# Low halves of split weights on VectorE, gates and residual queued behind the normalised operand, key transposes ahead of the compressed keys

## The chip, the cores and the metric

The kernel runs on one core of a Trainium2 chip. The metric is the device time of one execution in microseconds (us), here the median of three.

## The reference, cut to what matters

Two models in a row act on 256 tokens of width 1024. The first has two layers of feed-forward, mixer (three kinds of attention heads side by side) and feed-forward; the second has one layer of a mixer of state-space and short-convolution branches ("part 2" here), and a mixture of 16 experts.

```python
for l in range(2):
    x = x + 0.5 * swiglu(rmsnorm(x, ffn1_norm[l]), ffn1_wg[l], ffn1_wu[l], ffn1_wd[l])
    h = rmsnorm(x, mix_norm[l]) @ w_in[l]
    ...
    x = x + concat(mla(h_a), nsa(h_b), diff(h_c)) @ w_out[l]
    x = x + 0.5 * swiglu(rmsnorm(x, ffn2_norm[l]), ffn2_wg[l], ffn2_wu[l], ffn2_wd[l])
x = rmsnorm(x, final_norm)
...
proj = rmsnorm(concat(meta, x), norm_mix) @ w_in_2      # z, xBC, dt, b, c, h
h = h + concat(ssd(z, xBC, dt), short_conv(b, c, h)) @ w_out_2
h = h + hier_moe(rmsnorm(h, norm_ffn), ...)
return rmsnorm(h, norm_final)[:, 16:]
```

Here `swiglu` is silu(x wg) times (x wu), times wd.

## The kernel before, in words

**Split weights.** The results are wanted at float32 accuracy. A weight unit of up to 1 MB is fetched by SyncE into a tile `st` (`load`, four buffers) and split in two halves of up to 128 x 1024 elements (`split`, L154 to L170). For each, ScalarE writes a high half `wh` (L167), and then VectorE or GpSimd writes the low half `wl` = `st` - `wh` (L168); six buffers each. TensorE multiplies with both (`mm`, `mm2`, `mm3`; all their matmuls carry line L99). The two letters of the argument `lo` say which engine makes the low halves: "v" VectorE, "p" GpSimd. The table `LOW` and some literals in the calls set it.

**Operands.** An activation operand is made the same way: a high part on ScalarE, a low part on VectorE (`operand`, L268 and L269). Squares for the norm are summed up along the way (`squares`: L281 on ScalarE, L286 and L288 on VectorE); `sum_squares` puts their sums over the partitions into `pss` by TensorE, and `inv_rms` and `rsqrt` (L299, L124 to L131) make `rr` of it in a chain of twelve short VectorE instructions.

**The mixer of the first model.** It begins with the operand of the feed-forward's output, the matmuls of w_in's nine units (`w_in_groups`), and the norms of the latent (`ckvn`, L634, then its transposes `ckvt`). `nsa_prepare` makes compressed keys and values (`kcmp`, `vcmp`, from `h1`, L780) and the transposed queries and keys (`qtb`, `ktb`, copied to `ks` and `kw`). The heads follow, and then w_out: four units in two halves each, a psum bank each, and two additions to `xT` (L957). Psum banks go by tag: here S has 3, T 2, O 1 and W 2.

**Part 2.** A string `PART2` sets the order in which the pieces are written: "z10" multiplies two of four units of z, "u" makes the norms and the operand `u` (`u_operand`: L1106 scales, ScalarE makes the high part, L1108 the low part), "z2" and "z3" the other two units, "d" the decays, "b0" to "b3" and "x0" to "x3" the units whose products go through a short convolution (`conv`: ScalarE L1195, three times L1197 on VectorE, tanh on ScalarE, L1200), "r" rewrites the residual (`residual_norm`, L1112). The gates of z (`z_gates`) are read out of psum by ScalarE, put through tanh (L1095), and finished on VectorE (L1096). The chain of the decays ends with L1169, for which the matmul `acp` waits. Later `y_norm` (L1366, L1371) and w_out_2's units w0 to w7 follow, with the first experts' weights prefetched between.

**What sets the order.** The programs of the engines are written piece by piece, and a scheduler of the tile framework orders each engine's instructions by its own estimate of when they can run. Between the engines only data and buffers make waits. `behind` (L138) tells the scheduler to issue what is inside after a given instruction.

Of the kernel before, what the change touches and what calls it, by code (L numbers as in the profile page):

```python
# [10 lines left out]
F32 = mybir.dt.float32  # L11
# [7 lines left out]
T = 256  # L19
NM = 16  # L20
# [14 lines left out]
         "h0 s1 s1 g0 s1 s2 s2 n0 c1 h1 s2 s3 g1 n1 s3 c2 h2 g2 s3 "  # L35
         "| c3 h3 p5 g3 n2 y a w6 t0 t1 p7 t2 w0 n3 t3 % w1 p4 w5 w2 w4 p5 w3 w7")

LOW = {k: "pp" for k in ["d", "b0", "b1", "b2", "b3", "x0", "x1", "x2", "x3", "w6", "w1", "w3"]
       + [(1, 0, 0, 1), (1, 0, 1, 0)]}
LOW.update({k: "vp" for k in ["h3", "g2"]})  # L40
ORDER = "w01 w5 w2 mp m0 m1 w8 w3 w4 w6 np w7 dp m2 m3 d0 d1 n0 n1 d2 d3 n2 n3 n4 n5 m4 df m5"

# [1 line left out]
class Block:  # L44
# [272 lines left out]
    def _ffn(self, l, which, xops, after, extra):  # L317
# [27 lines left out]
        def gu(g, units):  # L345
            ps = []
            if g == 0 and not finish:

                ws = [w for u in units for w in self.split(u, "n")]
                ps = [self.bank(tag, "gu") for tag in "BBCC"]  # L350
                for k, i in ([(k, i) for k in range(4) for i in range(4)]
                             + [(k, i) for i in range(4) for k in range(4, KD)]):
                    self.mm2(ps[i], ws[i][0][:, k], ws[i][1][:, k], xhl[:, k], k == 0, k == KD - 1)
                return ps
            for i, u in enumerate(units):
                for f, (wh, wl) in enumerate(self.split(u, "n", LOW.get((which, l, g, i), "vv"))):
                    p = self.bank("BC"[i], "gu")
                    ps.append(p)
                    if finish and g == 0:

                        o = p[:, 0:T]
                        for n, (w, x) in enumerate(((wh, xh), (wh, xl), (wl, xh))):
                            for k in range(KD):
                                self.mm(p[:, T:2 * T] if n == 1 else o, w[:, k], x[:, k], n == k == 0, n == 2 and k == KD - 1)
                        continue
                    for k in range(KD):
                        self.mm2(p, wh[:, k], wl[:, k], xhl[:, k], k == 0, k == KD - 1)
            return ps
# [21 lines left out]
            return hx  # L390

        def down(g, hx, u):
            w = self.split(u, "k", LOW.get((which, l, g, 2), "vv"))
            for b in range(4):
                for j in range(2):
                    o = acc[b][:, j * T:(j + 1) * T]
                    c = (2 * b + j) * 128
                    for k in range(2):
                        wh, wl = w[k]
                        self.mm3(o, wh[:, 0, c:c + 128], wl[:, 0, c:c + 128], hx[:, k, 0], hx[:, k, 1],  # L400
                                 g == 0 and j == 0 and k == 0, g == NG - 1 and j == 1 and k == 1)
                if g == NG - 1:
                    xv = self.xT[:, 2 * b:2 * b + 2].rearrange("p j t -> p (j t)")
                    nc.vector.scalar_tensor_tensor(xv, acc[b], 0.25, xv, op0=OP.mult, op1=OP.add)  # L404
                    after(b)
# [107 lines left out]
    def _mixer(self, l, xops, after):  # L513
# [76 lines left out]

        def w_in_groups(ids):

            ws = [self.split(units[i], "k", {2: "pp", 3: "pp", 4: "vp", 5: "vp"}.get(i, "vv")) for i in ids]
            ps = [self.bank(tags.pop(0) if tags else "W", "win") for _ in ids]
            for k0 in range(KD):
                for k, i, t in ([(k0, i, t) for i in range(len(ids)) for t in range(2)] if len(ids) > 1 else
# [155 lines left out]
        def nsa_prepare():  # L752
# [24 lines left out]
            for i in range(2):  # L777
# [1 line left out]
                nc.scalar.activation(h1[q, 0], p[q, i * 30:(i + 1) * 30], AF.Tanh, scale=0.5)  # L779
                nc.vector.scalar_tensor_tensor(h1[q, 1], h1[q, 0], 1.0, p[q, i * 30:(i + 1) * 30],  # L780
                                               op0=OP.add, op1=OP.mult)
            p, p2 = self.bank("T", "kcmp"), self.bank("S", "vcmp")
            vcmp = ap.tile([16, 128], F32, name="vcmp", tag="vcmp")
            for g in range(2):
                self.mm(p[g * 64:(g + 1) * 64, 0:15], w2[0:64], h1[0:64, 1, g * 15:(g + 1) * 15])
                self.mm(p2[0:15, g * 64:(g + 1) * 64], h1[64:128, 1, g * 15:(g + 1) * 15], w2[64:128], g == 0, True)


            ks = ap.tile([128, 2, 16 + T], F32, name="ks", tag="hA")
            kw = ap.tile([128, 2, T], F32, name="kw", tag="cqT")  # L790
            nc.gpsimd.memset(ks, 0.0)
            nc.gpsimd.memset(kw, 0.0)
            for g in range(2):
                ACT(ks[g * 64:(g + 1) * 64, g, 0:15], p[g * 64:(g + 1) * 64, 0:15], scale=0.5)
            ACT(vcmp[0:15], p2[0:15, 0:128], scale=0.5)

            qT = ap.tile([128, 3, T], F32, name="qT", tag="qT")
            p, p2, p3 = self.bank("T", "qtb"), self.bank("T", "qtb"), self.bank("S", "ktb")
# [8 lines left out]
            for g in range(2):  # L807
                q = slice(g * 64, (g + 1) * 64)
                nc.vector.tensor_copy(ks[q, g, 16:16 + T], p3[q, 0:256])
                nc.vector.tensor_copy(kw[q, g], p3[q, 256:512])  # L810

            th = ap.tile([128, 2, 18], F32, name="gth", tag="gth")
            nc.scalar.activation(th, hV[:, :, 384:402], AF.Tanh, scale=0.5)
# [134 lines left out]
        KO = [int(c) for c in "01345672"]  # L948
        wo = [self.cols(a["w_out"][l], (b * 256, b * 256 + 256)) for b in range(4)]
        for b in range(4):  # L950
            for j, (wh, wl) in enumerate(self.split(wo[b], "n", {}.get(b, "vv"))):
                p = self.bank("W", "wo")
                for k in KO:
                    self.mm2(p, wh[:, k], wl[:, k], ohl[:, k], k == KO[0], k == KO[7])
                xv = self.xT[:, 2 * b + j]
# [66 lines left out]
    def _part2(self, xops):  # L1022
# [80 lines left out]
        def u_operand():  # L1103
            for k in range(KD):
                u = ap.tile([128, T], F32, name="u", tag="q", bufs=4)
                nc.vector.scalar_tensor_tensor(u, self.xT[:, k], self.gfm[:, k:k + 1], rb[:, 1], op0=OP.mult, op1=OP.mult)  # L1106
                ACT(uh[:, k, NM:], u)
                nc.vector.tensor_sub(ul[:, k, NM:], u, uh[:, k, NM:].bitcast(F32))  # L1108

        def residual_norm():  # L1110
            for k in range(KD):
# [282 lines left out]
        def run():  # L1394
            parts = decays()
            for name in steps:
                k, i = name[0], int(name[1:] or 0)
                if k == "z":
                    zs = z_blocks([int(c) for c in name[1:]])
                    if len(zs[0]) == 1:  # L1400
                        z_gates(*zs)
                elif k == "u":
                    norms()
                    u_operand()
                    z_gates(*zs)
                elif k == "r":
                    residual_norm()
                elif k == "d":
                    next(parts)
                elif k == "b":  # L1410
# [468 lines left out]
```

## Time and profile before

| | before |
|---|---|
| median of three executions | 1592.82 us |
| lowest and highest | 1591.33, 1594.35 us |
| profiled execution, its own time | 1591.45 us |
| its span | 1589.7 us |
| mean granted clock of TensorE | 0.984 |
| TensorE matmuls (PE) busy | 1527.9 us, 96% |
| VectorE (DVE) busy | 1046.6 us, 66% |
| ScalarE (ACT) busy | 733.9 us, 46% |
| GpSimd (POOL) busy | 170.7 us, 11% |
| moved by DMA | 308.91 MB, 194 GB/s |

The profile lists engines by short names: PE is TensorE's matmuls, PEld its weight loads, DVE VectorE, ACT ScalarE, POOL GpSimd. Lines are lines of the kernel before, unless said otherwise. A matmul wait is read from the list of waits: who waited, for whom, the sum in us, how many times, the longest. A timeline row gives start, duration, engine, line, operation, tiles and shapes, how many in a row, and in brackets the idle time before and what ended it. Busy time on VectorE and GpSimd includes time in which an instruction has started and stands still. The granted clock PEclk is a share of full speed; at half speed TensorE runs at 1.2 GHz, at full at 2.4.

### The profile page before, as it was taken

To read this page: it belongs to the slowest core of one execution; us is meant where nothing else is said; L and a number is where in the kernel's file an instruction comes from. 1 tells how busy PE (TensorE), PEld (TensorE's weight loads), DVE (VectorE), ACT (ScalarE), POOL (GpSimd) and SP (SyncE) were. 2 spreads that over 40 slices of the span, in tenths; PEclk is the share of its full clock that TensorE was granted. 3 is DMA by queue.
4 is the path that set the end of the run, shared out by engine and by line. 5 is a ranking of instruction groups with operands and counts; after the bars stand their busy time and mean duration, and the time that the engine had idled before them with its cause. 6 is when DMAs were issued, how large, how long until landed. Compare 5 with 4: busy or idle time off the path is not lost. (4 is left out here: it accounts for less than half of the span.)

```text
span 1589.7 us, 25210 instructions
## 1 busy us (share of the span) xinstructions
PE 1527.9 (96%) x9842; PEld 1266.7 (80%) x9842; DVE 1046.6 (66%) x1988; ACT 733.9 (46%) x1385; POOL 170.7 (11%) x174
## 2 busy tenths in 40 slices
PE   7999989999999999998999999999799999999996
PEld 6999988768999989998887799999799987444342
DVE  7777774868677786778467687778798875221122
ACT  5455455645554554455556455456554443010111
POOL 3000031330000000001115000001620122000000
PEclk9999999999999999999999999999899999999999
DMA  7756644205565555555440356555443479799993
GB/s 239 223 187 192 186 133 146 81 27 184 178 195 186 186 185 187 186 186 166 132 147 1 107 188 197 194 181 190 152 133 107 153 299 350 290 396 392 393 394 125
DMA packets 223557, 308.91 MB, mean 194 GB/s; under 512 B 20908, under 2 KB 167608, under 8 KB 223432
## 3 DMA queue, kind: packets, MB, share of 16 engines
q1 hardware_dynamic: 223128, 306.71, 57.8%
q8 instruction: 79, 1.29, 0.3%
q10 hardware_dynamic: 304, 0.53, 0.1%
q14 instruction: 46, 0.38, 0.1%
HBM read 306.16 MB, written 1.05 MB: 193 GB/s over the span
## 5 line engine op out<-in xcount | busy, mean ns | idle before, releaser
L167 ACT ACTIVATE wh<-st 128x1024 fp32r<-128x1024 f32 (+1 forms) x382 | 400.1, 1060 | 355.4 <-PE gu L99 116.8
L168 DVE TENSOR_TENSOR wl<-st,wh 128x1024 fp32r<-128x1024 f32 (+1 forms) x340 | 413.2, 1226 | 207.0 <-ACT wh L167 200.1
L99 PE MATMUL gu<-xhl,wh 128*128 128x512 f32 (+1 forms) x1440 | 492.1, 391 | 3.9 <-ACT wh L167 2.2
L99 PE MATMUL gu<-xhl,wl 128*128 128x256 f32 x1408 | 388.3, 279 | 0.0
L99 PEld LDWEIGHTS gu<-xhl,wh 128*128 128x128 f32 x1440 | 267.3, 189 | 63.1 <-ACT wh L167 3.5
L99 PEld LDWEIGHTS gu<-xhl,wl 128*128 128x128 f32 x1408 | 263.5, 189 | 0.1
L99 PE MATMUL acc<-hx,wh 128*128 128x256 f32 x1408 | 252.1, 281 | 0.0
L99 PEld LDWEIGHTS acc<-hx,wh 128*128 128x128 f32 x1408 | 216.2, 188 | 1.7
L168 POOL TENSOR_TENSOR wl<-st,wh 128x1024 fp32r<-128x1024 f32 (+1 forms) x42 | 102.6, 2461 | 1015.0 <-ACT wh L167 772.3
L99 PE MATMUL acc<-hx,wl 128*128 128x256 f32 x704 | 196.9, 281 | 0.0
L99 PE MATMUL proj<-uhl,wh 128*128 128x272 f32 (+2 forms) x592 | 131.0, 311 | 8.3 <-DVE uhl L1108 6.1
L99 PEld LDWEIGHTS acc<-hx,wl 128*128 128x128 f32 x704 | 132.6, 188 | 0.0
L99 PE MATMUL win<-wh,xhl 128*128 128x256 f32 (+1 forms) x576 | 111.1, 291 | 0.2 <-DVE xT L404 0.2
L99 PEld LDWEIGHTS proj<-uhl,wh 128*128 128x128 f32 x592 | 98.5, 196 | 13.7 <-DVE uhl L1108 6.8
L99 PE MATMUL proj<-uhl,wl 128*128 128x272 f32 (+2 forms) x328 | 96.5, 294 | 0.0
L99 PEld LDWEIGHTS win<-wh,xhl 128*128 128x128 f32 x576 | 93.5, 198 | 1.8 <-issue 1.1
L99 PE MATMUL win<-wl,xhl 128*128 128x256 f32 (+1 forms) x288 | 84.7, 294 | 0.0
L388 ACT ACTIVATE hx<-up 128x512 fp32r<-128x512 f32 x44 | 27.8, 632 | 94.3 <-DVE up L387 94.3
L99 PEld LDWEIGHTS proj<-uhl,wl 128*128 128x128 f32 x328 | 64.0, 195 | 0.2
L723 POOL TENSOR_SCALAR P<-P,mx 128x128 f32<-128x128 f32 (+2 forms) x88 | 54.3, 633 | 84.1 <-DVE mx L716 68.0
L99 PEld LDWEIGHTS win<-wl,xhl 128*128 128x128 f32 x288 | 56.9, 198 | 2.9 <-issue 2.7
L1776 DVE SCALAR_TENSOR_TENSOR ys<-y,rc,ys 128x512 fp32r<-128x512 f32 x16 | 11.7, 749 | 67.2 <-ACT ys L1593 66.8
(522 smaller groups left out, 2243.1 us busy)
## 6 DMA issues: line engine op xcount, KB each, us to landing
st<-ffn_wg SPq DMA_DIRECT2D x44, 1024.0 KB, 5.4
st<-ffn_wu SPq DMA_DIRECT2D x44, 1024.0 KB, 5.4
st<-ffn_wd SPq DMA_DIRECT2D x44, 1024.0 KB, 4.9
st<-w_in SPq DMA_DIRECT2D x36, 1024.0 KB, 5.4
st<-w_out SPq DMA_DIRECT2D x16, 1024.0 KB
mf<-expert_w_gate SPq DMA_DIRECT2D x25, 512.0 KB, 9.4
mf<-expert_w_down SPq DMA_DIRECT2D x21, 512.0 KB, 10.7
mf<-expert_w_up SPq DMA_DIRECT2D x18, 512.0 KB, 11.2
```

The lines of the kernel that those rows point to most:

```text
L99: return self.nc.tensor.matmul(out, lhsT, rhs, start=start, stop=stop, skip_group_check=True)
L167: hi = self.nc.scalar.activation(hl[0], src, AF.Copy)
L168: sub = (self.nc.gpsimd if lo[i] == "p" else self.nc.vector).tensor_sub(hl[1], src, hl[0].bitcast(F32))
L388: nc.scalar.activation(hh, up, AF.Copy)
L723: (nc.gpsimd if key + str(i) in "c0 c1 c2 d0 d1 m0 w0 w1".split() else nc.vector).tensor_scalar(P[:, d], P[:, d], r[:, i:i + 1], None, op0 ...
L1776: V.scalar_tensor_tensor(yl, py[half], rc[:, 1:2], yh.bitcast(F32), op0=OP.mult, op1=OP.subtract)
```

## The change

1. Low halves move from GpSimd to VectorE: of two units at the start of the first feed-forward (the up weights of its first group, the gate weights of its second), of w_in's units 2 to 5 in both mixers, and of d, b0, b1, b2, w6, w1 and w3 in part 2. That is 30 of 42 low halves on GpSimd (two of them of 512 columns); b3, x0 to x3, h3 and g2 keep theirs.
2. In `nsa_prepare` the matmuls of `kcmp` and `vcmp`, and ScalarE's copies of them, stand behind the transposes of queries and keys.
3. The second half of each w_out unit takes a psum bank of tag S in place of W.
4. `u_operand` returns its last low part; the gates of z and the residual's rewriting are issued behind it.

```diff
@@ -35,8 +35,7 @@
          "h0 s1 s1 g0 s1 s2 s2 n0 c1 h1 s2 s3 g1 n1 s3 c2 h2 g2 s3 "
          "| c3 h3 p5 g3 n2 y a w6 t0 t1 p7 t2 w0 n3 t3 % w1 p4 w5 w2 w4 p5 w3 w7")
 
-LOW = {k: "pp" for k in ["d", "b0", "b1", "b2", "b3", "x0", "x1", "x2", "x3", "w6", "w1", "w3"]
-       + [(1, 0, 0, 1), (1, 0, 1, 0)]}
+LOW = {k: "pp" for k in ["b3", "x0", "x1", "x2", "x3"]}
 LOW.update({k: "vp" for k in ["h3", "g2"]})
 ORDER = "w01 w5 w2 mp m0 m1 w8 w3 w4 w6 np w7 dp m2 m3 d0 d1 n0 n1 d2 d3 n2 n3 n4 n5 m4 df m5"
 
@@ -353,7 +352,7 @@
                     self.mm2(ps[i], ws[i][0][:, k], ws[i][1][:, k], xhl[:, k], k == 0, k == KD - 1)
                 return ps
             for i, u in enumerate(units):
-                for f, (wh, wl) in enumerate(self.split(u, "n", LOW.get((which, l, g, i), "vv"))):
+                for f, (wh, wl) in enumerate(self.split(u, "n", "vv")):
                     p = self.bank("BC"[i], "gu")
                     ps.append(p)
                     if finish and g == 0:
@@ -390,7 +389,7 @@
             return hx
 
         def down(g, hx, u):
-            w = self.split(u, "k", LOW.get((which, l, g, 2), "vv"))
+            w = self.split(u, "k", "vv")
             for b in range(4):
                 for j in range(2):
                     o = acc[b][:, j * T:(j + 1) * T]
@@ -590,7 +589,7 @@
 
         def w_in_groups(ids):
 
-            ws = [self.split(units[i], "k", {2: "pp", 3: "pp", 4: "vp", 5: "vp"}.get(i, "vv")) for i in ids]
+            ws = [self.split(units[i], "k") for i in ids]
             ps = [self.bank(tags.pop(0) if tags else "W", "win") for _ in ids]
             for k0 in range(KD):
                 for k, i, t in ([(k0, i, t) for i in range(len(ids)) for t in range(2)] if len(ids) > 1 else
@@ -779,20 +778,12 @@
                 nc.scalar.activation(h1[q, 0], p[q, i * 30:(i + 1) * 30], AF.Tanh, scale=0.5)
                 nc.vector.scalar_tensor_tensor(h1[q, 1], h1[q, 0], 1.0, p[q, i * 30:(i + 1) * 30],
                                                op0=OP.add, op1=OP.mult)
-            p, p2 = self.bank("T", "kcmp"), self.bank("S", "vcmp")
-            vcmp = ap.tile([16, 128], F32, name="vcmp", tag="vcmp")
-            for g in range(2):
-                self.mm(p[g * 64:(g + 1) * 64, 0:15], w2[0:64], h1[0:64, 1, g * 15:(g + 1) * 15])
-                self.mm(p2[0:15, g * 64:(g + 1) * 64], h1[64:128, 1, g * 15:(g + 1) * 15], w2[64:128], g == 0, True)
 
 
             ks = ap.tile([128, 2, 16 + T], F32, name="ks", tag="hA")
             kw = ap.tile([128, 2, T], F32, name="kw", tag="cqT")
             nc.gpsimd.memset(ks, 0.0)
             nc.gpsimd.memset(kw, 0.0)
-            for g in range(2):
-                ACT(ks[g * 64:(g + 1) * 64, g, 0:15], p[g * 64:(g + 1) * 64, 0:15], scale=0.5)
-            ACT(vcmp[0:15], p2[0:15, 0:128], scale=0.5)
 
             qT = ap.tile([128, 3, T], F32, name="qT", tag="qT")
             p, p2, p3 = self.bank("T", "qtb"), self.bank("T", "qtb"), self.bank("S", "ktb")
@@ -808,6 +799,14 @@
                 q = slice(g * 64, (g + 1) * 64)
                 nc.vector.tensor_copy(ks[q, g, 16:16 + T], p3[q, 0:256])
                 nc.vector.tensor_copy(kw[q, g], p3[q, 256:512])
+            p, p2 = self.bank("T", "kcmp"), self.bank("S", "vcmp")
+            vcmp = ap.tile([16, 128], F32, name="vcmp", tag="vcmp")
+            for g in range(2):
+                self.mm(p[g * 64:(g + 1) * 64, 0:15], w2[0:64], h1[0:64, 1, g * 15:(g + 1) * 15])
+                self.mm(p2[0:15, g * 64:(g + 1) * 64], h1[64:128, 1, g * 15:(g + 1) * 15], w2[64:128], g == 0, True)
+            for g in range(2):
+                ACT(ks[g * 64:(g + 1) * 64, g, 0:15], p[g * 64:(g + 1) * 64, 0:15], scale=0.5)
+            ACT(vcmp[0:15], p2[0:15, 0:128], scale=0.5)
 
             th = ap.tile([128, 2, 18], F32, name="gth", tag="gth")
             nc.scalar.activation(th, hV[:, :, 384:402], AF.Tanh, scale=0.5)
@@ -948,8 +947,8 @@
         KO = [int(c) for c in "01345672"]
         wo = [self.cols(a["w_out"][l], (b * 256, b * 256 + 256)) for b in range(4)]
         for b in range(4):
-            for j, (wh, wl) in enumerate(self.split(wo[b], "n", {}.get(b, "vv"))):
-                p = self.bank("W", "wo")
+            for j, (wh, wl) in enumerate(self.split(wo[b], "n")):
+                p = self.bank("WS"[j], "wo")
                 for k in KO:
                     self.mm2(p, wh[:, k], wl[:, k], ohl[:, k], k == KO[0], k == KO[7])
                 xv = self.xT[:, 2 * b + j]
@@ -1105,7 +1104,8 @@
                 u = ap.tile([128, T], F32, name="u", tag="q", bufs=4)
                 nc.vector.scalar_tensor_tensor(u, self.xT[:, k], self.gfm[:, k:k + 1], rb[:, 1], op0=OP.mult, op1=OP.mult)
                 ACT(uh[:, k, NM:], u)
-                nc.vector.tensor_sub(ul[:, k, NM:], u, uh[:, k, NM:].bitcast(F32))
+                low_u = nc.vector.tensor_sub(ul[:, k, NM:], u, uh[:, k, NM:].bitcast(F32))
+            return low_u.ins
 
         def residual_norm():
             for k in range(KD):
@@ -1398,13 +1398,16 @@
                 if k == "z":
                     zs = z_blocks([int(c) for c in name[1:]])
                     if len(zs[0]) == 1:
-                        z_gates(*zs)
+                        with self.behind(done):
+                            z_gates(*zs)
                 elif k == "u":
                     norms()
-                    u_operand()
-                    z_gates(*zs)
+                    done = u_operand()
+                    with self.behind(done):
+                        z_gates(*zs)
                 elif k == "r":
-                    residual_norm()
+                    with self.behind(done):
+                        residual_norm()
                 elif k == "d":
                     next(parts)
                 elif k == "b":
```

Lines of the changed kernel up to `nsa_prepare` are one lower than before (L168 is now L167).

The first place is VectorE before the first mixer's `pss`, with the squares of the last two column blocks. Before, from the fourth output block of the feed-forward on:

```order
L269 SCALAR_TENSOR_TENSOR xhl<-xT,v_1109,xhl 128x256
L286 TENSOR_TENSOR sq<-sq 128x512
L168 TENSOR_TENSOR wl<-st,wh 128x1024
L269 SCALAR_TENSOR_TENSOR xhl<-xT,v_1109,xhl 128x256 x2
L286 TENSOR_TENSOR sq<-sq 128x512
L269 SCALAR_TENSOR_TENSOR xhl<-xT,v_1109,xhl 128x256 x2
L286 TENSOR_TENSOR sq<-sq 128x512
L288 TENSOR_TENSOR sq<-sq 128x256
L299 TENSOR_SCALAR rrv<-pss 128x2
```

After:

```order
L268 SCALAR_TENSOR_TENSOR xhl<-xT,v_1109,xhl 128x256
L285 TENSOR_TENSOR sq<-sq 128x512
L167 TENSOR_TENSOR wl<-st,wh 128x1024
L268 SCALAR_TENSOR_TENSOR xhl<-xT,v_1109,xhl 128x256 x2
L285 TENSOR_TENSOR sq<-sq 128x512
L167 TENSOR_TENSOR wl<-st,wh 128x1024
L268 SCALAR_TENSOR_TENSOR xhl<-xT,v_1109,xhl 128x256 x2
L285 TENSOR_TENSOR sq<-sq 128x512
L167 TENSOR_TENSOR wl<-st,wh 128x1024
L287 TENSOR_TENSOR sq<-sq 128x256
L167 TENSOR_TENSOR wl<-st,wh 128x1024
L298 TENSOR_SCALAR rrv<-pss 128x2
```

Two more low halves (L167) stand ahead of the last sum of squares (L287), and a third between it and the reader of `pss` (L298).

The second place is VectorE in part 2, from the norm's copy `rb` on. Before, from where the low parts of `u` begin:

```order
L1108 TENSOR_TENSOR uhl<-u,uhl 128x256 x4
L1106 SCALAR_TENSOR_TENSOR u<-xT,gfm,rb 128x256
L1096 SCALAR_TENSOR_TENSOR z<-zth,z 128x256
L1106 SCALAR_TENSOR_TENSOR u<-xT,gfm,rb 128x256
L1096 SCALAR_TENSOR_TENSOR z<-zth,z 128x256
L1106 SCALAR_TENSOR_TENSOR u<-xT,gfm,rb 128x256 x2
L1112 SCALAR_TENSOR_TENSOR xT<-xT,v_1109,rb 128x256 x2
L1108 TENSOR_TENSOR uhl<-u,uhl 128x256
L1096 SCALAR_TENSOR_TENSOR z<-zth,z 128x256
L1112 SCALAR_TENSOR_TENSOR xT<-xT,v_1109,rb 128x256
L1108 TENSOR_TENSOR uhl<-u,uhl 128x256
L1112 SCALAR_TENSOR_TENSOR xT<-xT,v_1109,rb 128x256
```

After, from the first scaled `u` on:

```order
L1105 SCALAR_TENSOR_TENSOR u<-xT,gfm,rb 128x256 x4
L167 TENSOR_TENSOR wl<-st,wh 128x1024
L1107 TENSOR_TENSOR uhl<-u,uhl 128x256 x4
L1105 SCALAR_TENSOR_TENSOR u<-xT,gfm,rb 128x256 x3
L167 TENSOR_TENSOR wl<-st,wh 128x1024
L1105 SCALAR_TENSOR_TENSOR u<-xT,gfm,rb 128x256
L167 TENSOR_TENSOR wl<-st,wh 128x1024
L1107 TENSOR_TENSOR uhl<-u,uhl 128x256 x3
L167 TENSOR_TENSOR wl<-st,wh 128x1024
L1107 TENSOR_TENSOR uhl<-u,uhl 128x256
L1095 SCALAR_TENSOR_TENSOR z<-zth,z 128x256 x2
L1112 SCALAR_TENSOR_TENSOR xT<-xT,v_1109,rb 128x256 x8
```

All low parts of `u` (L1107) now come ahead of the gates (L1095) and the residual (L1112), and low halves of the weights stand between.

## Rows read from the trace of the kernel before

**Rows 1.** The list of PE's waits: who, for whom, us, times, longest.
```profile
PE pss L99 <- DVE sq L288: 9.2, 2, 4.8
PE proj L99 <- DVE uhl L1108: 6.1, 3, 3.8
...
PE acc L99 <- DVE rr L131: 2.6, 1, 2.6
PE btok L1217 <- DVE BC L1200: 2.2, 2, 1.5
...
PE wo L99 <- DVE xT L957: 1.9, 2, 0.9
PE kcmp L99 <- DVE h L780: 1.8, 2, 0.9
PE ckvt L641 <- DVE ckvn L634: 1.8, 2, 0.9
...
PE proj L99 <- DVE dv L1157: 1.7, 1, 1.7
...
PE yT L1297 <- DVE y L1371: 1.5, 1, 1.5
PE acp L99 <- DVE dv L1169: 1.2, 1, 1.2
```

**Rows 2.** Line L168 by engine: count, ns min/median/max, first and last start.
```profile
L168 DVE TENSOR_TENSOR wl<-st,wh x340: 1159/1226/2079, 11.9 to 1326.1; 128x1024 fp32r<-128x1024 f32 x168, 128x968 fp32r<-128x968 f32 x2
...
L168 POOL TENSOR_TENSOR wl<-st,wh x42: 1290/2412/4383, 13.8 to 1320.7; 128x1024 fp32r<-128x1024 f32 x40, 128x512 fp32r<-128x512 f32 x2
```

**Rows 3.** Timeline of VectorE at the first mixer's start: start us, duration us.
```profile
207.83 0.88 DVE L269 SCALAR_TENSOR_TENSOR xhl<-xT,v,xhl 128x256 fp32r<-128x256 f32 x2
208.62 0.69 DVE L286 TENSOR_TENSOR sq<-sq 128x512 f32<-128x512 f32 x1
209.23 5.17 DVE L269 SCALAR_TENSOR_TENSOR xhl<-xT,v,xhl 128x256 fp32r<-128x256 f32 x2
214.31 2.82 DVE L286 TENSOR_TENSOR sq<-sq 128x512 f32<-128x512 f32 x1
```

**Rows 4.** Timeline of GpSimd in the same stretch.
```profile
208.89 7.70 POOL L168 TENSOR_TENSOR wl<-st,wh 128x1024 fp32r<-128x1024 f32 x3 [183.45 <-ACT wh L167]
```

**Rows 5.** Timelines of VectorE and of GpSimd in the first feed-forward's start.
```profile
21.31 4.15 DVE L125 TENSOR_SCALAR nwy<-seed 128x2 int32<-128x2 int32 x1
...
13.83 9.79 POOL L168 TENSOR_TENSOR wl<-st,wh 128x1024 fp32r<-128x1024 f32 x4 [12.11 <-ACT wh L167]
```

**Rows 6.** Windows: length, busy PE, PEld, DVE, ACT, POOL, then PEclk, DMA share.
```profile
213.00:225.00 12.00, 7.65 (x39) 7.46 (x38) 6.91 (x16) 1.49 (x3) 3.59 (x2) 0.72 0.60 172
1113.00:1141.00 28.00, 20.56 (x128) 19.10 (x126) 20.34 (x32) 13.07 (x24) 17.69 (x7) 0.82 0.44 137
1141.00:1165.00 24.00, 19.66 (x145) 18.90 (x144) 23.48 (x50) 12.50 (x26) 13.82 (x6) 0.93 0.48 141
```

**Rows 7.** Timeline of VectorE in part 2.
```profile
1108.66 4.10 DVE L1106 SCALAR_TENSOR_TENSOR u<-xT,gfm,rb 128x256 f32<-128x256 f32 x4
...
1116.27 2.63 DVE L1106 SCALAR_TENSOR_TENSOR u<-xT,gfm,rb 128x256 f32<-128x256 f32 x1
1118.83 2.59 DVE L1096 SCALAR_TENSOR_TENSOR z<-zth,z 128x256 f32<-128x256 f32 x1
1121.34 0.47 DVE L1106 SCALAR_TENSOR_TENSOR u<-xT,gfm,rb 128x256 f32<-128x256 f32 x1
...
1124.33 2.58 DVE L1112 SCALAR_TENSOR_TENSOR xT<-xT,v,rb 128x256 f32<-128x256 f32 x1
...
1128.57 0.76 DVE L1096 SCALAR_TENSOR_TENSOR z<-zth,z 128x256 f32<-128x256 f32 x2
1134.93 1.57 DVE L1197 SCALAR_TENSOR_TENSOR cv<-proj,v,cv 128x271 f32<-128x271 f32 x3 [5.61 <-ACT cv L1195]
...
1158.07 2.13 DVE L1169 SCALAR_TENSOR_TENSOR dv<-dv,hb 128x48 f32<-128x48 f32 x1
```

## The prediction

> **What bounds the kernel now.** I read the list of PE's waits first, then the line of the low halves by engine, then the timelines of VectorE and GpSimd around the longest waits, and last the windows with the granted clock. PE is the engine to follow: what it waits for is the time that a change on other engines can win. Its waits are few and lie in few places [rows 1]: 9.2 us in two waits for the last sum of squares (L288) at the starts of the two mixers, 6.1 us in three waits for the normalised operand of part 2 (L1108), 2.6 us for rr in the first feed-forward, then a tail of 0.9 to 2.2 us each. In all these places the releaser is VectorE.
>
> Why is VectorE late there, when it is idle for a third of the span? A low half (L168) costs 1.226 us on VectorE and 2.412 us on GpSimd at the median, but the largest on VectorE is 2.079 and on GpSimd 4.383 [rows 2]. The timeline shows the other side [rows 3]: a pair of L269 takes 0.88 us at 207.83 and 5.17 us at 209.23; L286 takes 0.69 us at 208.62 and 2.82 us at 214.31. Between these, at 208.89, GpSimd began three low halves that ran for 7.70 us [rows 4]. So while GpSimd subtracts, an instruction of VectorE can be held for about one GpSimd instruction. That is not a matter of size: at 21.31 a shift of two numbers per partition took 4.15 us, inside a GpSimd stretch of four low halves [rows 5].
>
> The wait for L288 costs twice. In the window around the first mixer start the granted clock is 0.72 of full [rows 6]: PE stood still, and part of what followed ran at 1.2 instead of 2.4 GHz. Half speed in a share s of the window gives a mean of 1 - s/2, so at 0.72 PE loses 12 x 0.28 = 3.4 us beside the wait.
>
> **The change part by part.** Thirty low halves leave GpSimd: 30 x 2.41 = 72 us there, and 30 x 1.226 = 36.8 us more on VectorE [rows 2]. Loads, ScalarE's high halves and the matmuls stay the same in number. What counts is where those 36.8 us stand, and which held instructions come free. In each place:
>
> *Start.* The four low halves at 13.83 no longer hold the rr chain [rows 5]. The chain then ends before PE asks, since one of its instructions alone gives back 4 us: -2.6, the whole wait [rows 1]; bounds 0 and -2.6.
>
> *Mixer starts (two).* By the new order, two low halves stand before the last L288 (a third before the pss sums' reader): 2 x 1.23 = 2.5 us paid. Given back: 5.17 - 0.88 = 4.3 and 2.82 - 0.69 = 2.1, 6.4 us. So L288 comes 3.9 us earlier, against waits of 4.4 and 4.8. The pss matmuls also stand some 20 matmuls later on PE, which covers the rest. Both waits go (-9.2), and with them the slow clock (-3.4 each, taken the same in the second mixer): -16.0. Bounds: 0 (rr, two low halves later in the chain, is waited for instead) and -16.0.
>
> *The latent's norm (ckvt).* No GpSimd low half runs beside that chain any more, and its transposes stand later on PE: -1.8 [rows 1]; bounds 0 and -1.8.
>
> *Key transposes ahead of kcmp.* They fill PE's wait for h (1.8 in two), but now VectorE has four copies of ks and kw to do between the two L780, so vcmp waits about as long as kcmp did. 0; bounds -1.8 and +1.8, the wait's own size either way.
>
> *w_out's banks.* The second half's products go to S, so the wait for xT (1.9 in two) goes; in exchange several products end together, and VectorE adds them up in a burst just before the next feed-forward's first low halves. One to two low halves late (1.2 to 2.5 us per mixer) against 0.95 gained: +0.8 per mixer, +1.6 in all; bounds -1.9 and +3.1.
>
> *Part 2.* Its waits here are 6.1 + 2.2 + 1.7 + 1.2 = 11.2 us [rows 1], and the clock takes 28 x 0.18 = 5.0 us in the first window and 24 x 0.07 = 1.7 in the second [rows 6]: 17.9 us at most. Not all of it can go, since the convolutions behind the operand are paced by VectorE. I follow that queue [rows 7]. The last gate of z ended at 1128.57 + 0.76 = 1129.3. Held before it: four L1106 took 4.10 where one takes 0.47 (2.2), then 2.63, 2.59 and 2.58 where the shape takes about 0.47 (6.4 together): 8.6 us come back, since b0 to b2 leave GpSimd. Added from the first L1106 on are five low halves (6.1 us), and four gates go behind (1.6). VectorE is therefore ready for the first convolution at 1129.3 - 8.6 + 6.1 - 1.6 = 1125.2 in place of 1134.93, 9.7 us earlier. Placing the gates and the residual behind the last low part of u only helps: PE waits for u (L1108), nobody soon for them, and the banks of z are read by ScalarE, not by the gates. From there to the end of L1169, at 1160.2, VectorE took 25.3 us; four gates more make 26.9, so L1169 ends at 1152.1, 8.1 us earlier. GpSimd keeps b3 and x0 to x3, ten low halves in this stretch, now closer together; half a held instruction more takes 1.1. So -7; bounds 0 (VectorE held as long as before) and -17.9.
>
> *y_norm.* w6, w1 and w3 leave GpSimd; the wait for y goes, three more low halves in the chain stand against two long holds there: -1.5; bounds 0 and -1.5.
>
> Sum: -2.6 - 16.0 - 1.8 + 0 + 1.6 - 7 - 1.5 = -27.3 us. The profiled execution took 1591.45 us (1589.7 span, 1.75 around it), 1.37 below the median, so 1564.2 on its own scale and **1565.5** on the median's. The smallest difference that a measurement of this kernel can tell from none is about 0.2%, 3.2 us.
>
> **The rivals.**
> *(a) The convolutions set part 2's end as now.* GpSimd's ten remaining low halves hold VectorE as often, so the 9.7 us are used up before L1169. For it: VectorE was busy 23.48 of 24 us in that window [rows 6]. Then 1565.5 + 7 = 1572.5.
> *(b) rr is late in place of pss.* At the mixer starts VectorE puts two low halves into the chain to rr (+2.5 us), and PE comes there 7.8 us earlier. If PE finds no other work, half of the 16 us returns: 1573.5; with (a) 1580.5.
> *(c) All of part 2 comes free.* VectorE's holds shrink with fewer neighbours: 17.9 in place of 7: 1554.6.
> *(d) VectorE becomes the bound: slower.* The long instructions would not be GpSimd's doing but VectorE's own queue; nothing is then given back, and low halves before the awaited instructions are paid: two at each mixer start (4.9), five whole and two half-sized ones before the last u (7.4), one or two in the start's chain (2.5), 14.8 in all: 1607.6. It decides from the point where a held instruction gives back less than 1.23 us per low half moved; at the mixer start the rows give 6.4 for two [rows 3]. The Trainium skill, Perfetto Trace Analysis, section Optimizing Scalar/DVE Operations, speaks for (d): where VectorE is saturated, handing work to another engine may make sense; by that the sum would be this +14.8. The same paragraph adds that between VectorE and GpSimd it might not help, and 5.17 against 0.88 us is that case.
> *(e) The gain is returned in the experts' stage,* where transfers are dense: 1592.8, no change. Against it: no wait of PE for an expert's transfer is in the list, and the first expert transfers are issued in part 2 and move up with it.
>
> **How the numbers follow.** Forecast 0.55, (a) 0.14, (b) with or without (a) 0.13, (c) 0.08, (d) 0.06, (e) 0.04. Forecast to (c) are faster: 0.90; (e) is the same, 0.04; (d) slower, 0.06. The range takes in (c) below and (a) with (b) above, with 2 us for the w_out term: 1554 to 1583; (d) and (e) are left out.
>
> **What would show it.** Right: no wait of PE for L287 (the old L288) and clock 1.00 at both mixer starts; L285 and L268 at 0.69 and 0.44 us there; no wait for the last low part of u over 1 us; waits for btok, the decays and acp left between 1125 and 1160. Wrong: a new wait of PE for rr or for a low half on VectorE at 215 to 240, a wait of over 2 us at the first gu after w_out, or a low half on VectorE that is itself over 2 us where GpSimd is idle.

## The result and the profile after

The changed kernel takes **1576.36 us** (median of four executions, 1575.87 to 1578.37) against 1592.63 us of the kernel before (1591.33 to 1594.35, four executions). The ratio is 0.990, with a 95% interval of 0.9882 to 0.9917: about 1.0% or 16 us faster. The forecast was 1565.5 us, with a range of 1554 to 1583. The profiled execution's span is 1574.1 us.

First the line of the page with the busy time of each engine in the kernel after, its share of the span and the number of instructions.

```profile
PE 1521.3 (97%) x9842; PEld 1261.7 (80%) x9842; DVE 1033.6 (66%) x2018; ACT 732.0 (46%) x1385; POOL 96.9 (6%) x144
```

GpSimd's busy time has fallen from 170.7 to 96.9 us. VectorE has 30 instructions more, at 1.226 us each some 37 us of work, and yet its busy time has fallen too, from 1046.6 to 1033.6 us. So some 50 us of what counted as busy before were time in which an instruction stood still.

Now the list of PE's waits in the kernel after, with the columns of [rows 1].

```profile
PE gu L98 <- DVE xT L956: 11.2, 4, 3.6
PE proj L98 <- DVE cv L1197: 5.1, 2, 4.2
...
PE vcmp L98 <- DVE h L779: 1.9, 2, 1.0
...
PE acp L98 <- DVE dv L1169: 1.0, 1, 1.0
```

The three leading waits of [rows 1] are no longer there: 9.2 us for the sum of squares, 6.1 for the operand `u`, 2.6 for `rr`. In their place stand two that were not in the list before: 11.2 us in four waits of `gu` for `xT`, and 5.1 us in two for `cv`.

The mixer's start answers to [rows 3, 4]. VectorE's timeline of the kernel after:

```profile
205.96 0.87 DVE L268 SCALAR_TENSOR_TENSOR xhl<-xT,v,xhl 128x256 fp32r<-128x256 f32 x2
206.75 0.68 DVE L285 TENSOR_TENSOR sq<-sq 128x512 f32<-128x512 f32 x1
207.35 1.22 DVE L167 TENSOR_TENSOR wl<-st,wh 128x1024 fp32r<-128x1024 f32 x1
208.49 0.42 DVE L287 TENSOR_TENSOR sq<-sq 128x256 f32<-128x256 f32 x1
```

Both kinds of instructions now take what they take alone, 0.87 us for two L268 and 0.68 us for one L285. The last sum of squares starts at 208.49, with two low halves more before it.

The windows of the kernel after, with the columns of [rows 6]: the mixer's start and the stretch behind w_out.

```profile
206.00:218.00 12.00, 12.00 (x104) 12.00 (x104) 8.67 (x24) 5.85 (x11) 0.00 (x0) 1.00 0.75 199
351.00:363.00 12.00, 6.58 (x24) 5.05 (x23) 10.39 (x20) 4.67 (x8) 0.00 (x0) 0.72 0.80 262
```

At the mixer's start the granted clock is 1.00 and PE is busy throughout. Behind w_out it is 0.72: that loss has moved from the one place to the other.

If one looks up the same matmuls in both timelines, the time gained so far can be read at the ends of the stages. The table is worked out from these starts and ends.

| stage, to which matmul | gained by its end | in this stage | forecast |
|---|---|---|---|
| start and first feed-forward, last `gu` | 4.4 us | 4.2 | 2.6 |
| first mixer, first `wo` | 14.4 | 10.0 | 8.9 |
| first w_out and the feed-forwards behind it, last `gu` | 8.1 | -6.4 | -0.8 |
| second mixer, first `wo` | 18.8 | 10.8 | 8.9 |
| second w_out and feed-forward | 11.7 | -7.1 | -0.8 |
| part 2 to the first `segs` | 17.1 (after 18.4 at `acp`) | 5.4 | 7.0 |
| y_norm to the last `vt` and `yT` | 18.9 | 1.8 | 1.5 |
| experts, last matmul | 16.6 | -2.3 | 0 |

(The forecast's 16.0 for the mixer starts and 1.8 for the latent's norm are put half to each mixer. 0.2 us were gained before the first feed-forward, and 1.0 us is lost behind the last matmul.)

Most terms were met, but for one: w_out, forecast to lose 1.6 us in all, lost 13.5. The timelines show how. PE, around the end of w_out in the kernel after:

```profile
351.16 0.39 PE L98 MATMUL gu<-xhl,wh 128*128 128x512 f32 x1
...
355.59 0.74 PE L98 MATMUL gu<-xhl,wh 128*128 128x512 f32 x1 [3.57 <-DVE xT L956]
...
358.38 0.77 PE L98 MATMUL gu<-xhl,wh 128*128 128x512 f32 x1 [1.84 <-DVE xT L956]
```

And VectorE in the same place; L955 and L956 add w_out's products to `xT`, L268 makes the next operand:

```profile
341.50 0.77 DVE L955 TENSOR_TENSOR xT<-wo,xT 128x256 f32<-128x256 f32 x2 [3.17 <-PE wo L98]
...
349.71 0.47 DVE L268 SCALAR_TENSOR_TENSOR xhl<-xT,v,xhl 128x256 fp32r<-128x256 f32 x1
...
355.03 0.41 DVE L956 TENSOR_TENSOR xT<-wo,xT 128x256 f32<-128x256 f32 x1
...
357.83 0.41 DVE L956 TENSOR_TENSOR xT<-wo,xT 128x256 f32<-128x256 f32 x1
...
361.00 0.42 DVE L287 TENSOR_TENSOR sq<-sq 128x256 f32<-128x256 f32 x1
```

w_out's last product ends at 351.3, but VectorE adds from 341.5 on without a break, and ends the next operand and its squares only at 361.4. The first column block that `gu` lacks is added at 355.03, the next at 357.83. PE waits 5.4 us in two pieces here and 5.8 us in the second layer. In the kernel before, VectorE waits for w_out instead, product by product:

```profile
361.07 0.48 DVE L269 SCALAR_TENSOR_TENSOR xhl<-xT,v,xhl 128x256 fp32r<-128x256 f32 x1
361.77 0.42 DVE L956 TENSOR_TENSOR xT<-wo,xT 128x256 f32<-128x256 f32 x1 [0.22 <-PE wo L99]
362.23 0.42 DVE L957 TENSOR_TENSOR xT<-wo,xT 128x256 f32<-128x256 f32 x1
...
364.61 0.42 DVE L956 TENSOR_TENSOR xT<-wo,xT 128x256 f32<-128x256 f32 x1 [0.23 <-PE wo L99]
```

### The profile page after: what moved, and what is told of

It is laid out like the page before. It is cut to its first block, busy times and chain, and to the rows that moved or that the text cites. A ratio compares the mean times of both kernels' runs of the same rounds, so it can differ in the third digit from the quotient of the medians.

```text
span 1574.1 us, 25194 instructions
## 1 busy us (share of the span) xinstructions
PE 1521.3 (97%) x9842; PEld 1261.7 (80%) x9842; DVE 1033.6 (66%) x2018; ACT 732.0 (46%) x1385; POOL 96.9 (6%) x144
## 4 chain that ended last, share of the span: by engine, by line
PE 91%; DVE 6%; ACT 1%; issue 1%; DMA 0%; POOL 0%; ACTq 0%; DVEq 0%
PE gu L98 31%; PE acc L98 16%; PE proj L98 7%; PE win L98 6%; PE gate L98 4%; PE y L98 4%; PE up L98 4%; PE h L98 3%; PE S L98 3%; PE opair L98 2%; PE wo L98 2%; PE zp L98 1%; DVE wl L167 1%; PE ptp L683 1%; PE moe L98 1%; PE xgp L98 1%
## 5 line engine op out<-in xcount | busy, mean ns | idle before, releaser
L167 DVE TENSOR_TENSOR wl<-st,wh 128x1024 fp32r<-128x1024 f32 (+1 forms) x370 | 447.4, 1219 | 214.1 <-ACT wh L166 202.9
L98 PE MATMUL gu<-xhl,wh 128*128 128x512 f32 (+1 forms) x1440 | 496.9, 394 | 14.3 <-DVE xT L956 11.2
L712 ACT ACTIVATE P<-S,mx 128x256 f32<-128x256 f32 (+2 forms) x128 | 49.1, 397 | 17.4 <-DVE nwy L130 3.8
## 6 DMA issues: line engine op xcount, KB each, us to landing
mf<-expert_w_up SPq DMA_DIRECT2D x18, 512.0 KB, 11.2
```

The lines of the kernel that those rows point to most:

```text
L98: return self.nc.tensor.matmul(out, lhsT, rhs, start=start, stop=stop, skip_group_check=True)
L167: sub = (self.nc.gpsimd if lo[i] == "p" else self.nc.vector).tensor_sub(hl[1], src, hl[0].bitcast(F32))
L712: nc.scalar.activation(P[:, d], s[:, c], AF.Exp, bias=m[:, 0, i:i + 1], accum_out=m[:, 1, i:i + 1])
```

## The experiments

Theory A, formed on these rows: the banks of tag S let w_out's products run ahead during the attention, so that less of PE's work stands beside VectorE's additions, low halves and operand parts, and the next feed-forward waits. The rival, B: VectorE is late there since it now makes more low halves in the mixer. Of the other parts it was open which of them made the gains, and whether GpSimd's subtractions hold VectorE or only stand where it is late.

**e1: w_out's banks as before.**

```diff
-                p = self.bank("WS"[j], "wo")
+                p = self.bank("W", "wo")
```

> The changed kernel with w_out's products all on banks of tag W again; the other parts of the change stay. Theory A (the S banks let w_out's products run ahead and end together, so that VectorE's additions to xT come in a burst that the next feed-forward's first matmuls wait for): the waits of gu for xT (11.2 us in four) and the half clock behind them (2 x 3.4 us) go, the two waits of wo for xT (0.9 us each) come back: 13 to 16 us less than the changed kernel, 1560 to 1564 us. Theory B (the burst comes from the low halves that VectorE now makes in the mixer, whatever the banks): waits of gu for xT of over 3 us per layer stay, 1573 to 1578 us.

Measured: 1564.33 us, ratio to the kernel before 0.9805 (0.9782 to 0.9829). The waits of `gu` for `xT` are gone, and the waits for `xT` in w_out are back:

```profile
PE wo L98 <- DVE xT L956: 1.9, 2, 0.9
```

A holds: 12 us of the change's gain were lost in w_out by the medians, 15 by the ratios (the kernel before took 2.4 us longer in these rounds). The profiled executions of the two kernels differ by 13.9 us between the first `wo` and the last `gu` behind it, both layers together.

**e2: the S banks alone,** in the kernel before (the same line the other way).

> The kernel before with the second half of each w_out unit on a bank of tag S, and nothing else of the change. Theory A: two new groups of waits of gu for xT of about 5 us each with half clock behind them, 13 to 16 us slower than before: 1605 to 1609 us. Theory B: no such waits, 1590 to 1594 us.

Measured: 1607.97 us, ratio 1.0076 (1.0059 to 1.0092), slower by 0.8%. The waits are those of the kernel after:

```profile
PE gu L99 <- DVE xT L957: 10.8, 4, 3.6
```

The window behind the first w_out, with the columns of [rows 6], has a granted clock of 0.57:

```profile
370.00:382.00 12.00, 8.10 (x27) 6.67 (x28) 7.88 (x16) 2.57 (x5) 0.00 (x0) 0.57 0.60 184
```

So the loss needs nothing else of the change, and B falls: VectorE's low halves in this kernel's mixers are those of before. The size by the ratio is 12 us (9 to 15), as in e1.

**e3: the thirty low halves alone,** in the kernel before.

```diff
-LOW = {k: "pp" for k in ["d", "b0", "b1", "b2", "b3", "x0", "x1", "x2", "x3", "w6", "w1", "w3"]
-       + [(1, 0, 0, 1), (1, 0, 1, 0)]}
+LOW = {k: "pp" for k in ["b3", "x0", "x1", "x2", "x3"]}
...
-            ws = [self.split(units[i], "k", {2: "pp", 3: "pp", 4: "vp", 5: "vp"}.get(i, "vv")) for i in ids]
+            ws = [self.split(units[i], "k") for i in ids]
```

> The kernel before with the thirty low halves moved to VectorE, and nothing else of the change. If low halves on GpSimd hold VectorE's instructions, the start (4.4 us by the two traces), both mixer starts (20.8 us) and y_norm (1.6 us) come whole, part 2 gives 0 to 6: 1559 to 1567 us, no wait of PE for the sum of squares. If instead the order of the queues (the other parts of the change) made these gains, or VectorE is the bound: 1580 to 1607 us.

Measured: 1560.48 us, ratio 0.9787 (0.9770 to 0.9803); again in more rounds (e12, the same kernel) 1560.65 us and 0.9788 (0.9775 to 0.9802). This is the whole gain, and more than the change as a whole keeps: **2.1%**.

> The kernel of e3 again, on the chip of e9 to e11 and in more rounds, to set them beside it: 1559 to 1563 us.

**e4: the queueing behind the operand alone,** in the kernel before (the diff's part in `u_operand` and `run`).

> The kernel before with the gates of z and the residual's rewriting queued behind the last low part of u, and nothing else of the change. If GpSimd's low halves are what holds the operand back, PE still waits 2 to 4 us for it in place of 6.1, and the convolutions' pace stays: 1589 to 1592 us. If the place of the gates makes part 2's gain (5.6 us between the two traces): 1585 to 1588 us. If the gates' wait moves to someone behind them: over 1594 us.

Measured: 1593.76 us, ratio 0.9993 (0.9981 to 1.0006): no effect. The wait for the operand falls to 2.9, but another comes, for the tanh of z on ScalarE:

```profile
PE proj L99 <- DVE uhl L1108: 2.9, 1, 2.9
PE proj L99 <- ACT zth L1095: 2.8, 1, 2.8
```

**e5: GpSimd subtracts for nothing.** VectorE's queue is that of e3. In both mixers GpSimd makes w_in's six low halves a second time, into a tile that nobody reads; the results are the same.

```diff
+            if lo[i] == "d":
+                twin = self.ap.tile([128, 4, T], F32, name="twin", tag="kC0")
+                self.nc.gpsimd.tensor_sub(twin[:, :kk, :nn], src, hl[0].bitcast(F32))
...
-            ws = [self.split(units[i], "k") for i in ids]
+            ws = [self.split(units[i], "k", {2: "dd", 3: "dd", 4: "vd", 5: "vd"}.get(i, "vv")) for i in ids]
```

> The kernel of e3 (thirty low halves on VectorE, nothing else of the change), and in both mixers GpSimd subtracts w_in's six halves once more into a tile that nobody reads, where it made them in the kernel before. The results don't depend on it, VectorE's queue and work are those of e3. If GpSimd's subtractions hold VectorE's instructions, L285 or L268 at the mixer starts take over 2 us again, PE waits for the last sum of squares again (4 to 9 us, since VectorE also has the low halves), and 18 to 30 us of e3's gain are lost: 1578 to 1592 us. If the long instructions were made by the order of VectorE's queue, or by GpSimd's results being late: no change, 1558 to 1564 us.

Measured: 1574.75 us, ratio 0.9892 (0.9876 to 0.9909): 14 us of e3's gain are lost, less than the 18 to 30 expected, through work on which nothing depends. VectorE and GpSimd in e5 at the first mixer's start (L271 and L288 are L268 and L285 of e3):

```profile
207.09 5.19 DVE L271 SCALAR_TENSOR_TENSOR xhl<-xT,v,xhl 128x256 fp32r<-128x256 f32 x2
212.21 2.83 DVE L288 TENSOR_TENSOR sq<-sq 128x512 f32<-128x512 f32 x1
```

```profile
205.62 8.87 POOL L170 TENSOR_TENSOR twin<-st,wh 128x1024 f32<-128x1024 f32 x3 [202.98 <-ACT wh L166]
```

The same place in e3, with the same queue on VectorE:

```profile
207.07 0.88 DVE L268 SCALAR_TENSOR_TENSOR xhl<-xT,v,xhl 128x256 fp32r<-128x256 f32 x2
207.87 0.69 DVE L285 TENSOR_TENSOR sq<-sq 128x512 f32<-128x512 f32 x1
```

And PE's wait for the sum of squares is back in e5:

```profile
PE pss L98 <- DVE sq L290: 7.7, 2, 3.8
```

The 5.19 and 2.83 us are those of [rows 3], 5.17 and 2.82, within 0.02 us. Beside this wait only 1.0 us in two waits for `xhl` is new in e5's list. GpSimd's subtractions hold VectorE; neither the queue's order nor GpSimd's results do.

The Trainium skill, SBUF — State Buffer, section Who interferes with whom, describes such a hold: VectorE and GpSimd share a pair of ports as an exclusive lock, and an instruction of VectorE with two inputs in SBUF contends for it with one of GpSimd that reads SBUF. This case agrees: GpSimd's three instructions take 8.87 us here, and VectorE's stand still for 6.5 of them. By the same section an instruction with one input in SBUF, outside certain modes, isn't held; L1197, whose other input is a product in psum, took 0.51 us each at 1118.12 in the kernel after, while GpSimd was at work (shown further down).

**e6: no low half on GpSimd.** e3 with `LOW = {}`.

> The kernel of e3 with the remaining twelve low halves (b3, x0 to x3 whole, h3 and g2 by one half) on VectorE as well, so that GpSimd makes none. If GpSimd's ten low halves hold the convolutions' chain, part 2's waits (2.3 for the operand, 1.6, 1.4, 1.2, 0.8 behind it) fall below 4 us together: 1554 to 1559 us. If VectorE is the bound there (it takes 12 x 1.23 = 14.8 us more): the waits grow, 1562 to 1570 us.

Measured: 1560.62 us, ratio 0.9799 (0.9782 to 0.9815), beside e3's 0.9787: no gain. The `acp` of the decays comes at 1134.98 in e6 and at 1129.73 in e3, though no GpSimd instruction is there to hold anything: VectorE has more low halves ahead of it. The later convolutions more than make it up: between the last `gu` and the last `yT` e6 gains 10.4 us on the kernel before, e3 8.7. The profiled execution of e6 loses as much elsewhere, 1.0 and 1.4 us against e3 in the mixers and 1.1 in the experts; in each of these stages it has 3.4 us more at half clock.

**e7: low halves and key transposes.**

> The kernel of e3 with the key transposes moved up; no S banks, no queueing behind the operand. e3 took 1560.5 and the kernel of e1, which also queues behind, 1564.3. If the key transposes only exchange the wait for kcmp with one for vcmp: 1559 to 1562 us. If they cost, by a longer wait and the slow clock behind it: 1562 to 1566 us.

Measured: 1563.16 us (1560.25 to 1564.05), ratio 0.9815 (0.9799 to 0.9832). Its profiled span, 1558.3 us, is that of e3, 1558.4. The waits in the list change names, 1.8 us for `kcmp` against 1.9 for `vcmp`:

```profile
PE vcmp L98 <- DVE h L779: 1.9, 2, 1.0
```

Between none and 0.3% slower; these runs don't settle it.

**e8: low halves and the queueing behind.**

> The kernel of e3 with the gates of z and the residual's rewriting queued behind the operand; no S banks, key transposes where they were. If the eight instructions of the residual and four gates, now ahead of the convolutions in VectorE's queue, hold psum banks for PE (the 4.2 us wait of proj for cv): 2 to 4 us above e3, 1562 to 1565 us. If the queueing is without effect: 1559 to 1562 us.

Measured: 1564.21 us (1563.93 to 1565.68), ratio 0.9823 (0.9807 to 0.9839), above the interval of e12. The wait for the operand is gone, and the one for `cv` stands there as in the kernel after:

```profile
PE proj L98 <- DVE cv L1196: 5.1, 2, 4.2
```

Two more kernels say which of the two queued pieces costs.

**e9: the residual behind the convolutions.** e8 with the step "r" after "b3", behind the last BC:

```diff
-                    with self.behind(done):
+                    with self.behind(self.conved):
                         residual_norm()
```

> The kernel of e8 (thirty low halves moved, gates of z behind the operand) with the residual's rewriting queued behind the last BC of the convolutions in place of behind the operand. If the eight instructions of the residual (3.25 us) in front of the convolutions make the 4.2 us wait of proj for cv: that wait falls below 1.5 us, and the waits for the operand stay gone: 1557 to 1561 us. If the four gates and the low half there make it: 1562 to 1565 us as e8.

**e10: only the gates behind the operand,** the residual where the scheduler puts it, among the parts of `u`.

> The kernel of e8 with only the gates of z queued behind the operand; the residual goes where the scheduler puts it, among the parts of u. If the residual behind the operand is the costly part: 1559 to 1562 us, with a wait for the operand of some 2 us and none over 2 us for cv. If the gates are: 1562 to 1565 us.

Measured: e9 1563.91 us, 0.9805 (0.9790 to 0.9819); e10 1560.71 us, 0.9796 (0.9777 to 0.9814). In e9 the wait for `cv` falls from 4.2 to 2.0 at its longest, not below 1.5 as expected, and its time is that of e8. `acp` comes as early as in e3 (30.6 us ahead of the kernel before in both), and 4.6 us against e3 are lost from there to the last `yT`. The eight instructions now stand among the convolutions, beside two of GpSimd's last low halves:

```profile
1136.26 7.53 DVE L1112 SCALAR_TENSOR_TENSOR xT<-xT,v,rb 128x256 f32<-128x256 f32 x8
```

```profile
1136.90 2.49 POOL L167 TENSOR_TENSOR wl<-st,wh 128x1024 fp32r<-128x1024 f32 x1 [3.52 <-ACT wh L166]
1139.82 2.51 POOL L167 TENSOR_TENSOR wl<-st,wh 128x1024 fp32r<-128x1024 f32 x1 [0.42 <-ACT wh L166]
```

They take 7.53 us there, and 3.25 in the kernel after, where GpSimd is idle beside them. In e10 the wait for the operand is 0.9, that for `cv` 1.7, and the time is that of e3. So the residual behind the operand is the costly piece, some 3 us (between the last `gu` and the last `yT` e8 gains 6.3 us, e10 9.4 and e3 8.7), and the gates' queueing is worth nothing that the times tell.

**e11: e9 without any GpSimd half.**

> The kernel of e9 with GpSimd's last twelve low halves on VectorE too. If GpSimd's holds are what is left of part 2's waits: 2 to 5 us less than e9. If VectorE's own work is (12 x 1.23 = 14.8 us more): the same as e9 or up to 3 us more.

Measured: 1561.15 us, 0.9787 (0.9770 to 0.9803). That is 2.8 us less than e9, as expected if GpSimd's holds are what is left there, though the two intervals overlap. The residual takes its 3.24 us again:

```profile
1134.72 3.24 DVE L1111 SCALAR_TENSOR_TENSOR xT<-xT,v,rb 128x256 f32<-128x256 f32 x8
```

The time is within the intervals of e3, e6 and e10: none of these arrangements beats moving the thirty low halves and nothing else.

## Why the prediction was right, and where it was wrong

*The time.* The result is 10.9 us above the forecast. That it still lies in the range is luck in part: the upper end of the range had been drawn for (a) with (b), neither of which came (the list has no wait for `rr`, and part 2 gained most of its 7 us), and what took that room was w_out, with several times its bound. The sign of being wrong that names the first `gu` after w_out came, with 3.57 us; the signs of being right at the mixer starts came too.

*The cause.* VectorE was late because GpSimd held its instructions. e5 shows it directly, with VectorE's queue as in e3. Rival (d), that VectorE would become the bound, is excluded by e3, which has the 36.8 us on VectorE and nothing beside, and gains 2.1%. What was paid and given back is right too: at the first mixer's start the wait went and the clock stayed at 1.00.

*Start, mixers, y_norm.* Forecast 2.6, 17.8 and 1.5, found 4.2, 20.8 and 1.8. At the start I missed a second wait: right behind the one for `rr`, the next `gu` had waited 0.7 us for `gp`, and that went with it; what makes up the rest of the 4.2 is not traced. The lists of the kernel before and the kernel after:

```profile
PE gu L99 <- DVE gp L379: 1.6, 2, 0.9
```

```profile
PE gu L98 <- DVE gp L378: 0.9, 1, 0.9
```

Of the 20.8 us some 1.7 are luck: the profiled execution of the kernel before has 3.4 us at half clock near its second `kcmp` (0.86 from 821 to 833 us), the kernel after has none there. Such a stretch comes and goes between kernels: e6, e9 and e11 have it, e3 and e5 do not.

*Key transposes.* Forecast 0; by e7 and the list of waits they exchange one wait for another. Right within what the runs tell.

*w_out's banks.* This is the step that failed. I wrote "One to two low halves late (1.2 to 2.5 us per mixer)", and set the bound at 3.1 us; it was 13.5 by the stages, 12 by the medians of e1 and by e2. I had counted only low halves behind the last products. But each of w_out's eight products brings VectorE two additions, an operand part, half a sum of squares and a low half: in the kernel before L956 and L957 are 0.42 us each, L269 0.48, L168 1.23, L286 0.69 for two, 2.9 us together, and one product on PE took 2.8 us (from the addition at 361.77 to that at 364.61). The two kept step, and w_out's matmuls were the cover for VectorE's work. With three more banks PE did part of these matmuls earlier, in place of attention work that then came later; what it did early no longer covered anything. Of the first w_out's 128 matmuls 108 stand behind the last one of the attention in the kernel before, e1 and e3, and 78 in the kernel after and e2, which have the banks. VectorE's 20 us from 341.5 to 361.4 stood beside 10 us of w_out. The wait is then counted twice, as at the mixer's start, by the slow clock behind it: 12 x 0.28 = 3.4 us per layer.

*Part 2.* Forecast 7, found 5.4; with the low halves alone it is 7.1 (23.5 to 30.6 us ahead in e3). L1169 was to end 8.1 us earlier, and `acp`, which waits for it, gains 6.7 us in this stage (11.7 to 18.4); 1.3 of these are lost again behind it. The number came out better than its working. The 9.7 us set VectorE's readiness, 1125.2, against the start of the first convolution, 1134.93; but the row of that start says that VectorE had been free since 1129.3 and waited 5.61 us for ScalarE's `cv` [rows 7]. By its own terms VectorE came 4.1 us earlier, and why `cv` would come earlier too was not worked out. Two sentences of that step do not hold either. "Placing the gates and the residual behind the last low part of u only helps" is wrong: e8, e9 and e10 price the residual there at some 3 us. It pushes the gates of z into the stretch in which GpSimd makes b3 and x0. VectorE in the kernel after:

```profile
1107.45 0.76 DVE L1095 SCALAR_TENSOR_TENSOR z<-zth,z 128x256 f32<-128x256 f32 x2
1108.12 3.25 DVE L1112 SCALAR_TENSOR_TENSOR xT<-xT,v,rb 128x256 f32<-128x256 f32 x8
1111.29 0.76 DVE L1095 SCALAR_TENSOR_TENSOR z<-zth,z 128x256 f32<-128x256 f32 x2
...
1114.44 3.75 DVE L1095 SCALAR_TENSOR_TENSOR z<-zth,z 128x256 f32<-128x256 f32 x2 [0.76 <-ACT zth L1094]
1118.12 1.02 DVE L1197 SCALAR_TENSOR_TENSOR cv<-proj,v,cv 128x270 f32<-128x270 f32 x2
```

```profile
1112.77 7.65 POOL L167 TENSOR_TENSOR wl<-st,wh 128x1024 fp32r<-128x1024 f32 x3 [260.77 <-ACT wh L166]
```

Two gates at 1114.44 take 3.75 us, the convolution behind them comes at 1118.12, and PE, whose next product needs the bank that it frees, waits 4.24 us:

```profile
1119.29 0.49 PE L98 MATMUL proj<-uhl,wh 128*128 128x272 f32 x2 [4.24 <-DVE cv L1197]
```

I had said that nobody waits soon for the gates; what stands behind them in VectorE's queue does. And GpSimd's ten remaining halves still hold VectorE in this stretch: L1169 took 2.43 us at 1139.38 in the kernel after, beside a subtraction, and 0.19 in e9, where GpSimd was idle at that moment. Without them part 2 is shorter, by 1.7 us from e3 to e6 and by 5.1 from e9 to e11 in the profiled executions; that the whole kernel gains by it is not shown.

*The experts.* Rival (e) was given 4% as a whole; 2.3 us that were not in the sum were lost there, but not by its mechanism: 2.0 of them fall at one place, shown below, where it is the order of PE's instructions and not a transfer.

## What to carry to other kernels

Before moving work from a slow engine to a loaded one, look at what the slow engine does to the others' instructions while it runs: here 30 operations moved onto VectorE cost it 37 us and gave it back 50, and an unused copy of twelve of them on GpSimd takes away 14 of the 34 us that they gain. More psum banks are no free gain: they let TensorE run ahead, and matmuls done early cover nothing later; count everything that each product brings to the consumer, and compare it with the time of a product. And of a change in several parts, measure the parts alone: one of these gave 2.1%, one took back 0.8%, and one some 0.3%, which add up to about the 1.0% of the whole.

## What the runs showed of the hardware that I had not expected

A long hold repeats: with three subtractions of the same shape on GpSimd at the same place, VectorE's two L268 and one L285 took 5.17 and 2.82 us in the kernel before and 5.19 and 2.83 in e5, with different work behind them.

Matmuls of 64 columns go in pairs, until something stands between them. The experts' down product runs as two streams, and the timeline of the kernel before shows 14 matmuls in 3.22 us:

```profile
1545.48 3.22 PE L99 MATMUL y<-ms,acts 128*64 128x512 f32 x14
1548.64 0.44 PE L1718 MATMUL stp<-identr,slots 128*128 128x128 f32 x2
```

In the kernel after the last of them come singly, four of one stream, the first transpose of the next piece, then four of the other:

```profile
1526.61 3.17 PE L98 MATMUL y<-ms,acts 128*64 128x512 f32 x10
1529.71 0.33 PE L1721 MATMUL stp<-identr,slots 128*128 128x128 f32 x1
1529.97 1.93 PE L98 MATMUL y<-ms,acts 128*64 128x512 f32 x4
1531.83 0.33 PE L1721 MATMUL stp<-identr,slots 128*128 128x128 f32 x1
```

The single ones follow each other at 0.43 us, as the pairs do, so that four pairs take twice their time, and with it 2.0 us of the gain is gone. What separates the streams in these kernels is the order of PE's instructions, which the scheduler has changed: before, the last matmuls of one stream and of the other stand next to each other, ahead of both transposes; after, the first transpose stands between them. The 32 matmuls of this piece take 7.14 us in the kernel before, e2 and e4, which have the old order, 9.20 in the kernel after, e1, e3, e5 to e8 and e10 to e12, and 9.92 in e9, which has a third order. No run changed this order alone.
